# Decayed running sum behind a matmul: x's first two chunks loaded by halves of channels instead of halves of time

## The chip, the cores and the metric

The kernel runs on one core of a Trainium2 chip. The metric is the device time of one execution in microseconds, as the median of several runs. A core has five engines that work side by side, each through its own instructions in order: TensorE (PE, the matrix unit; PEld is its weight load), VectorE (DVE), ScalarE (ACT), GpSimd (POOL) and SyncE (SP). Transfers between the chip's main memory (HBM) and the core's memory (SBUF) are issued by some of these engines and carried out by 16 DMA engines. Matmul results go to PSUM, a memory of eight banks of 512 float32 columns for each of 128 partitions.

## The reference

```python
B, S, D = (16, 2048, 1024)            # x (B, S, D), w (D, D), decay (D), all float32
xw = x @ w
out[:, 0, :] = xw[:, 0, :]
for t in range(1, S):
    out[:, t, :] = decay[None, :] * out[:, t - 1, :] + xw[:, t, :]
```

So there are 16 independent sequences of 2048 steps. Each step is multiplied by a 1024 x 1024 matrix, and then a first-order recurrence with one decay for each output channel runs along time.

## The kernel before

**Chunks.** Time is cut into chunks of TL = 512 steps; there are 64 chunks in all. For each chunk the kernel forms the transposed product, with 128 output channels on the partitions and 512 steps along the row. Two chunks next to each other of one sequence make a group. A *step* (or slot) of the main loop is one group and one of the K = 8 blocks n of 128 output channels. It takes 2 x 8 matmuls of 128 x 128 weights by 512 columns, and its result fills a tile `ps` of 1024 columns (two PSUM banks). There are three such tiles, and two single banks called `spare`.

**Loading x.** The 1024 input channels are cut into NQ = 4 quarters of CQ = 256 channels. `load` (L101) fetches one quarter q of a chunk by a DMA on POOL's queue: 32 partitions (step modulo 32), NJ = 16 blocks of 32 steps, 256 channels. The DMA converts float32 to bf16 on the way. The tile `xb` holds the chunk with (quarter, step in the block) on the 128 partitions and (block j, channel) along the row. There are three `xb` tiles, used in turn, so the load of chunk c + 3 waits until chunk c has been transposed.

**Transposing x.** `turn` (L110) runs VectorE's 32 x 32 transpose over pairs of bf16 values taken as float32. The result `xw` has channel pairs on the partitions and is indexed [m, j, i, e]: m = 0 to 3 counts groups of channel pairs, (j, i) is the time, and e is the even or the odd channel of a pair. Contraction index k = 2m + e. `part` (L119) separates even and odd into `xt`, whose rows are contiguous in time; a matmul can also read `xw` directly with a stride of two (`pairs` in `matmul`, L125).

**Loading w.** `load_w` (L321) fetches w by half h of the output channels and parity e of the input channel, four DMAs each; `settle` (L328) and `settle_slots` (L376) copy it into `wsb` in the order that the matmuls want. Part (h, e) = (0, 0) comes first, over SP's and ACT's queues. The other three, called U0, U1, U2 here, go over POOL's queue.

**The order of the work.** Each engine works in the order in which the code records its instructions. A written agenda gives that order: entry -99 is the start, entries 0 to 33 follow steps 0 to 33, and later steps follow a rule. Each word of it is a letter and a number:

- M i loads half i of the first two chunks (M0 and M1 are chunk 0, M2 and M3 chunk 1), U i a part of w, and L the next quarter load from a list that starts with chunk 2 and grows by chunk c + 3 whenever chunk c is transposed.
- E i transposes one m of one half in time, and F i and G i copy it to `xt` on VectorE and on ACT: i = 0 to 3 is chunk 0's first half in time with m = 0 to 3, 4 to 7 its second half, and 8 to 15 the same for chunk 1.
- w i and W i settle a piece of w on ACT and on VectorE, q and Q on VectorE in two parts. K q copies one value of quarter q's load to a `gate` tile; warm-up matmuls that read the gate follow.
- T c transposes a whole later chunk; X c and Y c copy its m = 0, 1 and m = 2, 3 to `xt` on ACT.
- For a step s that is "paired": p and g copy its `ps` tile to SBUF on ACT (the whole to `xs`, and the even columns times decay to `h`), j adds on POOL, S scans on VectorE, h prepares the other half on ACT and c fills it in on POOL. `xs` has three buffers, so the p of the third paired step from then on waits for c. For a step that is not paired, S scans straight out of PSUM. B transposes a result for the store, which goes over SP's queue.

All of POOL's DMA issues share eight completion semaphores in turn, so that a load waits on POOL for the landing of the load eight places before it.

**The first steps.** Steps 0 to 3 are done together (L630 to L649). Chunk 0 goes into `firsts`, four banks: the four even k for the first half in time (256 columns), the same for the second half, and the odd k with 512 columns. Chunk 1 goes into `seconds` in two halves of 256 columns. From step 4 on all matmuls have 512 columns; step 8 (L669) does the blocks of steps 8 and 9 together.

Of the kernel before, what the change touches and what calls it, by code (L numbers as in the profile page):

```python
# [9 lines left out]
FP32 = mybir.dt.float32  # L10
BF16 = mybir.dt.bfloat16
# [3 lines left out]
def _ap(ap_obj: bass.AP, new_ap, extra_offset=0):  # L15
    return dataclasses.replace(
        ap_obj,
        ap=[list(p) for p in new_ap],
        offset=ap_obj.offset + extra_offset,
    )  # L20
# [5 lines left out]
def kernel(  # L26
# [26 lines left out]
    nc = tc.nc  # L53
    pin = tc.keep_in_program_order
    B, S, D = x.shape
# [3 lines left out]
    P = 32  # L59
    CQ = D // NQ  # L60
    K = CQ // P
    M = K // 2
    TL = 512
    NJ = TL // P
# [6 lines left out]
    sb = ctx.enter_context(tc.tile_pool(name="sb", bufs=1))  # L71
# [4 lines left out]
    def ring(pool, name, count, shape, dtype=FP32):  # L76
        i = turns[name] = turns.get(name, -1) + 1
        return pool.tile(shape, dtype, name=f"{name}{i % count}")

    def quad(q):  # L80
        return slice(q * P, (q + 1) * P)

    chunks = [(b, c * TL) for b in range(B) for c in range(NC)]
# [13 lines left out]
    xb_of = {}  # L97
    xw_of = {}
    xt_of = {}

    def load(c, q, j0=0, j1=NJ):  # L101
        b, t0 = chunks[c]
        if c not in xb_of:
            xb_of[c] = ring(sb, "xb", 3, [128, NJ, CQ], BF16)
        pin(nc.gpsimd.dma_start(  # L105
            out=xb_of[c][quad(q), j0:j1],
            in_=_ap(x, [[D, P], [P * D, j1 - j0], [1, CQ]],
                    (b * S + t0 + j0 * P) * D + q * CQ)))

    def turn(c, j0=0, j1=NJ, m0=0, m1=M):  # L110
        if c not in xw_of:
            xw_of[c] = ring(sb, "xw", 2, [128, M, NJ, P, 2], BF16)
        src = xb_of[c][:, j0:j1].rearrange("p j c -> p (j c)").bitcast(FP32)
        dst = xw_of[c].rearrange("p m j i e -> p (m j i e)").bitcast(FP32)
        pin(nc.vector.transpose(  # L115
            out=dst.rearrange("p (m j i) -> p j m i", m=M, i=P)[:, j0:j1, m0:m1],
            in_=src.rearrange("p (j m c) -> p j m c", m=M, c=P)[:, :, m0:m1]))
# [7 lines left out]
    def matmul(ps, n, k, xt, t0=0, t1=TL, start=0, pairs=None):  # L125
        if pairs is None:
            rhs = xt[:, k // 2, k % 2, t0:t1]
        else:
            rhs = pairs[:, k // 2, t0 // P:t1 // P, :, k % 2].rearrange("p j i -> p (j i)")
        lhs = wsb[:, k, n].rearrange("p q i -> p (q i)")  # L130
        pin(nc.tensor.matmul(  # L131
            out=ps[:, t0:t1] if ps.shape[1] >= t1 else ps,
            lhsT=lhs,
            rhs=rhs,
            start=(k == 0 and t0 == start),
            stop=(k == K - 1),
        ))
# [213 lines left out]
    H = NJ // 2  # L351
    halves = ((0, H), (H, NJ))
    for q in range(NQ):
        pin(nc.sync.dma_start(
            out=rows[q * P:q * P + R],
            in_=_ap(decay, [[P, R], [CH, 2], [1, P]], q * CR)))
    cols = const.tile([128, 2, P], FP32, name="cols")

    def load_half(i):
        for q in range(NQ):  # L360
            load(i // 2, q, *halves[i % 2])

    def spin_on(q):
        pin(nc.scalar.copy(out=gates[q][quad(q), 0:1], in_=xb_of[0][quad(q), 0, 0:1]))
# [44 lines left out]
    def bank(some, r, spot):  # L409
        both = psp.tile([128, len(some), NQ, 2, P], FP32, name=spot)  # L410
        for i in some:
            banks[i, r] = both, i - some[0]
# [22 lines left out]
    def half_slot(s, half, spot=None):  # L435
        tile_ = tiles[s % len(slots)]
        if spot is not None:
            tile_.ps.append(psp.tile([128, TL], FP32, name=spot)[:, 0:TL // 2])
        t = half * TL // 2
        for k in range(K):  # L440
            matmul(tile_.ps[half], tile_.n, k, xt_of[nch - 1], t, t + TL // 2, t)
# [35 lines left out]
    def turn_and_load(c):  # L477
# [44 lines left out]
        "L": lambda i: load(*loads.pop(0)) if loads else None,  # L522
    }
    agenda = {
        -99: "M0 M1 U0 M2 M3 U1 U2 w0 W1 w2 W3 K0 K1 K2 K3 E0 E1 G0 E2 G1 E3 F2 G3 E4 E5 G4 E6 G5 E7 F6 G7 q4 w5 Q4 W6 W7 D E8 E9 G8 E10 G9 E11 F10 G11 E12 L E13 G12 L E14 G13 E15 L F14 G15",
        0: "p0 z0 W8 W9 W10 W11",
        1: "g0",
        2: "L S1 L",
# [76 lines left out]
    def rest(s):  # L605
        do = [f"S{s - 1}"] if tiles[s - 1].paired else []
        do.append(f"C{s - 1}")
        if tiles[s - 2].paired:
            do.append(f"B{s - 2}")
        return do + [f"B{s - 1}"] + later.get(s, []) + ["L"] * len(loads)  # L610

    def perform(do):
        for deed in do:
            deeds[deed[0]](int(deed[1:] or 0))
# [3 lines left out]
    for step, (g, n) in enumerate(slots):  # L618
        T = TL * len(g)
        left = step - len(slots)  # L620
        if n % R == 0:
            ns, nj = range(n, n + R), T // P
            if left == -2 * R:
                outlets = [Outlet(ns, H, half) for half in range(2)]
            else:
                pieces = 1 if left < -7 * R else 2 if left < -6 * R else nj // H
                outlets = [Outlet(ns, nj, pieces=pieces, parts=2 if left == -5 * R else 1)]
        if left == -R:
            outlets = []
        if step == 0:  # L630
            heads = [ring(psp, "ps", 3, [128, T]) for _ in range(3)]
            firsts = [ps[:, 0:TL] for ps in heads] + [spares[0]]
            seconds = [ps[:, TL:T] for ps in heads] + [spares[1]]
            for j0, j1 in halves:
                for k in range(0, K, 2):
                    for i in range(R):
                        matmul(firsts[i], i, k, xt_of[0], j0 * P, j1 * P, pairs=xw_of[0])
            for k in range(1, K, 2):
                for i in range(R):
                    matmul(firsts[i], i, k, xt_of[0])  # L640
            for k0 in range(0, K, 2):
                for i in range(R):
                    for k in (k0, k0 + 1):
                        matmul(seconds[i], i, k, xt_of[1], 0, H * P,
                               pairs=xw_of[1] if k0 < 4 else None)
            for i in range(R):
                for k in range(K):
                    matmul(seconds[i], i, k, xt_of[1], H * P, TL, H * P,
                           pairs=xw_of[1] if i < 2 else None)  # L649
        if step < R:  # L650
            ps = heads[n] if n < 3 else tuple(spares)
        else:
            if step == K + 1:
                ps = nexts
            elif -R <= left < -1:
                ps = ring(psp, "ps", 3, [128, TL])
                spots.append(f"ps{turns['ps'] % 3}")
                if left == -2:
                    ps = [ps[:, 0:TL // 2]]
            elif len(g) == 2 or n % R < 3:  # L660
                ps = ring(psp, "ps", 3, [128, T])
            elif left == -1:
                ps = [ring(psp, "spare", 1, [128, TL])[:, 0:TL // 2]]
            else:
                ps = ring(psp, "spare", 1, [128, TL])
            todo = [(k, l) for k in range(K) for l in range(len(g))]
            if step < K:
                todo.sort(key=lambda kl: kl[0] % 2)
            elif step == K:  # L669
                todo = []  # L670
                nexts = (ring(psp, "spare", 1, [128, TL]), ring(psp, "ps", 3, [128, TL]))
                for l in range(len(g)):
                    for i, half in enumerate((ps[:, l * TL:(l + 1) * TL], nexts[l])):
                        for k in range(K):
                            matmul(half, n + i, k, xt_of.get(g[l]),
                                   pairs=xw_of[g[l]] if g[l] in (3,) else None)
            elif step == K + 1:
                todo = []
            if left >= -2:
                todo = []  # L680
            if 40 <= step < 190:
                pin(nc.tensor.nop(hint="x", nofuse=True))
            for k, l in todo:
                matmul(ps[:, l * TL:(l + 1) * TL], n, k, xt_of[g[l]])
        tiles.append(Tile(g, n, ps, outlets))
        if left >= -2:
            half_slot(left, 0)
        if left == -1:
            half_slot(-2, 1, spots[0])
            bank((0, 1), 0, "spare10")  # L690
        do = agenda.get(step, agenda.get(left) if left >= -20 else None)
        if do is None:
            do = usual(step)
        else:
            do = do.split()
            if left == -20:
                do = rest(step) + do
        perform(do)
# [29 lines left out]
```

## Time and profile before

| | |
|---|---|
| median of 3 runs | 903.84 us (903.73 to 904.28) |
| profiled execution, its own time | 903.68 us |
| span of its instructions | 901.9 us |
| granted TensorE clock | 1.00 |
| busy: PE, DVE, ACT, POOL | 892.0, 825.6, 687.6, 657.0 us |
| 512-column matmuls into `ps` from `xt` | 3934, mean 378 ns with overlap |
| x half loads (128 KB written) | 16, median 5.7 us to landing |
| x quarter loads (256 KB written) | 248, median 7.8 us to landing |
| w loads over POOL's queue | 12, median 5.1 us to landing |

A busy time counts overlapping matmuls once, while a mean of one matmul includes its overlap with its neighbours. The distance between two matmul starts is read from the chain. Sizes of transfers are those of the bf16 that is written, and the float32 that is read is twice as much. "Under 512 B" in the packet line counts the 4-byte completions as well.

In views of the chain and the timeline the columns are the start in us, the duration in us, and what ran; in the timeline the brackets tell how long the engine was idle before it and what ended that. In views of waits the numbers are the total in us, how often, and the longest. In the table of engines they are the busy time, its share of the span and the number of instructions.

### The profile page before, as it was taken

The page shows a single profiled execution, that of the slowest core. Times are in us where ns is not written, and L with a number is a line of the kernel's source. Part 1 is how long each engine was busy: PE and PEld are TensorE (multiplying, and loading weights), DVE is VectorE, ACT ScalarE, POOL GpSimd, SP SyncE. Part 2 cuts the span into 40 slices and gives each one's busy share as a digit, 9 for nine tenths or more (in the row PEclk, how much of TensorE's full clock was granted, in tenths as well). Part 3 has the DMA queues.
Part 4 walks back from the last instruction along what each step waited for, and adds up shares of the span by engine and source line. Part 5 has one row for each costly group of instructions (what it writes and reads, how often), then busy time and mean ns, then how long its engine had stood idle before and what let it go on. Part 6 is the DMA issues. An engine that isn't in the chain of part 4 may idle for free.

```text
span 901.9 us, 12226 instructions
## 1 busy us (share of the span) xinstructions
PE 892.0 (99%) x4127; PEld 412.1 (46%) x4209; DVE 825.6 (92%) x636; ACT 687.6 (76%) x962; POOL 657.0 (73%) x755
## 2 busy tenths in 40 slices
PE   9999999999999999999999999999999999999998
PEld 5544444444444444444444444444444444444444
DVE  4999999999999999999998999999999999999998
ACT  4889867777877877878778778777787787787743
POOL 7888678777767768777677687777777777776532
PEclk9999999999999999999999999999999999999999
DMA  9999999999999999999999999999999999999768
GB/s 193 196 215 217 231 218 217 215 240 253 254 249 252 248 249 252 242 247 230 225 234 228 224 228 228 233 228 228 232 229 228 227 230 225 228 226 222 176 152 234
DMA packets 403182, 204.77 MB, mean 227 GB/s; under 512 B 9392, under 2 KB 402096, under 8 KB 403120
## 3 DMA queue, kind: packets, MB, share of 16 engines
q1 hardware_dynamic: 265808, 134.77, 60.9%
q0 software_dynamic: 137024, 68.70, 56.7%
q8 instruction: 33, 0.54, 0.2%
q10 hardware_dynamic: 288, 0.52, 0.2%
q14 instruction: 29, 0.24, 0.1%
HBM read 138.42 MB, written 134.22 MB: 302 GB/s over the span
## 4 chain that ended last, share of the span: by engine, by line
PE 97%; DMA 1%; issue 1%; POOL 0%; DVE 0%; ACT 0%; DVEq 0%; POOLq 0%
PE ps L131 96%; PE spare L131 1%; DMA xb<-in_x_dram 1%; DMA ot<-in_w_dram 1%; POOL ot L323 0%; DVE so L233 0%; PE ps L419 0%; PE spare L419 0%; ACT xb L426 0%; DVE wsb L379 0%; DVEq L379 0%; POOLq L712 0%
## 5 line engine op out<-in xcount | busy, mean ns | idle before, releaser
L131 PE MATMUL ps<-xt,wsb 128*128 128x512 bf16 x3934 | 860.8, 378 | 4.7 <-DVE wsb L379 0.4
L131 PEld LDWEIGHTS <-wsb 128*128 128x128 bf16 x4160 | 406.8, 98 | 478.7 <-ACT wsb L330 0.8
L208 POOL TENSOR_TENSOR xs<-h,xs 128x512 f32<-128x512 f32 (+1 forms) x190 | 243.0, 1279 | 189.8 <-ACT h L169 84.6
L186 ACT COPY xs<-ps 128x1024 f32<-128x1024 f32 (+1 forms) x190 | 188.9, 994 | 156.9 <-PE ps L131 146.3
L283 DVE STREAM_TRANSPOSE ot<-so 128x1024 f32<-128x1024 f32 (+2 forms) x265 | 300.4, 1172 | 2.5 <-POOL so L202 1.1
L266 POOL TENSOR_TENSOR so<-h,xs 128x512 f32<-128x512 f32 (+1 forms) x190 | 241.5, 1273 | 41.2 <-ACT h L169 27.0
L123 ACT COPY xt<-xw 128x2048 bf16<-128x2048 bf16 (+1 forms) x136 | 242.3, 1790 | 7.6 <-DVE xw L115 7.4
L105 POOL DMA_DIRECT2D xb<-in_x_dram x264 | 174.3, 661 | 3.0 <-POOLq L712 0.9
L169 ACT ACTIVATE h<-so,dec 128x512 f32<-128x512 f32 (+1 forms) x190 | 145.4, 766 | 25.5 <-DVE so L213 22.3
L115 DVE STREAM_TRANSPOSE xw<-xb 128x2048 f32<-128x2048 f32 (+1 forms) x78 | 147.3, 1900 | 5.3 <-DMA xb<-in_x_dram 5.3
L213 DVE TENSOR_TENSOR_SCAN so<-spare,keep,xs 128x512 f32<-128x512 f32 (+1 forms) x97 | 120.0, 1240 | 27.6 <-POOL xs L208 27.2
L213 DVE TENSOR_TENSOR_SCAN so<-spare,xs 128x512 f32<-128x512 f32 x93 | 113.3, 1220 | 27.2 <-POOL xs L208 24.4
L169 ACT ACTIVATE h<-ps,dec 128x512 f32<-128x512 f32 (+1 forms) x189 | 129.5, 685 | 0.0
L233 DVE TENSOR_TENSOR_SCAN so<-dec,ps 128x1024 f32<-128x1024 f32 x34 | 76.9, 2261 | 0.8 <-ACT h L169 0.6
L233 DVE TENSOR_TENSOR_SCAN so<-dec,keep,ps 128x1024 f32<-128x1024 f32 (+2 forms) x35 | 74.8, 2140 | 0.0
L270 ACT COPY keep<-so 128x1 f32<-128x1 f32 x136 | 25.4, 189 | 9.1 <-DVE so L233 8.6
L204 ACT COPY so<-keep 128x1 f32<-128x1 f32 x97 | 18.4, 191 | 2.4 <-DVE ot L283 2.2
L131 PE MATMUL spare<-xt,wsb 128*128 128x512 bf16 (+1 forms) x64 | 12.9, 332 | 0.0
L131 PE MATMUL ps<-xw,wsb 128*128 128x256 bf16 (+1 forms) x68 | 11.2, 301 | 0.0
L202 POOL MEMSET so<- 128x1 f32 x93 | 10.7, 117 | 0.6 <-DVE ot L283 0.6
L323 POOL DMA_DIRECT2D ot<-in_w_dram x12 | 6.5, 546 | 3.2 <-DMA xb<-in_x_dram 1.9
L348 PE MATMUL spare<-idle 128*128 128x512 bf16 x22 | 6.8, 483 | 1.2 <-DVE idle L338 1.2
(40 smaller groups left out, 40.5 us busy)
## 6 DMA issues: line engine op xcount, KB each, us to landing
out_dram<-ot SPq DMA_DIRECT2D x236, 512.0 KB, 10.8
xb<-in_x_dram POOLq DMA_DIRECT2D x248, 256.0 KB, 7.8
out_dram<-ot SPq DMA_DIRECT2D x56, 128.0 KB, 2.6
xb<-in_x_dram POOLq DMA_DIRECT2D x16, 128.0 KB, 5.7
out_dram<-ot SPq DMA_DIRECT2D x8, 256.0 KB, 4.5
ot<-in_w_dram POOLq DMA_DIRECT2D x12, 128.0 KB, 5.1
out_dram<-xb SPq DMA_DIRECT2D x4, 256.0 KB
ot<-in_w_dram ACTq DMA_DIRECT2D x2, 256.0 KB, 5.1
```

Source lines behind the costliest of these rows:

```text
L105: pin(nc.gpsimd.dma_start(out=xb_of[c][quad(q), j0:j1], in_=_ap(x, [[D, P], [P * D, j1 - j0], [1, CQ]], (b * S + t0 + j0 * P) * D + q * CQ)))
L115: pin(nc.vector.transpose(out=dst.rearrange("p (m j i) -> p j m i", m=M, i=P)[:, j0:j1, m0:m1], in_=src.rearrange("p (j m c) -> p j m c", ...
L123: pin(copy(out=xt_of[c][:, m0:m1, :, j0 * P:j1 * P], in_=src))
L131: pin(nc.tensor.matmul(out=ps[:, t0:t1] if ps.shape[1] >= t1 else ps, lhsT=lhs, rhs=rhs, start=(k == 0 and t0 == start), stop=(k == K - 1),))
L169: pin(nc.scalar.activation(out=h, in_=src, func=mybir.ActivationFunctionType.Copy, scale=dec[:, self.n:self.n + 1]))
L186: pin(nc.scalar.copy(out=self.xs[:, i * size:(i + 1) * size], in_=ps))
L208: pin(nc.gpsimd.tensor_tensor(out=odds, in0=self.g, in1=odds, op=ALU.add))
L213: pin(nc.vector.tensor_tensor_scan(out=so[:, 3:T + 2:2], data0=squares[-1][:, n:n + 1].to_broadcast([128, T // 2]), data1=self.xs[:, 1:T:2 ...
L233: pin(nc.vector.tensor_tensor_scan(out=so[:, t + 2:t + 2 + size], data0=dec[:, n:n + 1].to_broadcast([128, size]), data1=ps, initial=befor ...
L266: pin(nc.gpsimd.tensor_tensor(out=self.so[:, 2:T + 2:2], in0=self.h, in1=self.xs[:, 0:T:2], op=ALU.add))
L270: pin(nc.scalar.copy(out=self.keep, in_=self.so[:, self.T + 1:self.T + 2]))
L283: pin(nc.vector.transpose(out=outlet.ot[:, j:j + size, c0:c0 + P], in_=self.so[:, t1:t1 + size * P].rearrange("p (i t) -> p i t", t=P)))
```

## The change

The first two chunks are cut in another direction. M0 loads channels 0 to 127 of each quarter for all 512 steps of chunk 0, and M1 channels 128 to 255. M2 and M3 do so for chunk 1. `load_side` takes the place of `load` for this; the tile is read as [side, j, channel] for these chunks, and `turn` takes its source from there. The sixteen DMAs carry the same bytes. Each row that is read is 512 B long instead of 1 KB, and there are twice as many.

The E, F and G of the agenda's entry -99 keep their number and size and get another order, since M0 now brings m = 0, 1 of both halves in time and M1 brings m = 2, 3. One L is added at the end of the entry, so that each later L takes the load that the next one took before.

The matmuls of steps 0 to 3 change from 96 with 256 columns and 16 with 512 to 8 with 256 columns (chunk 0, k = 0) and 60 with 512. Chunk 1 runs k = 0 to 3 for all four blocks out of `xw`, and then k = 4 to 7 block by block.

On ACT, VectorE and SP the kinds and the number of instructions stay as they are. On POOL the number stays, and the loads from chunk 2 on stand one place earlier among the other work.

```diff
--- before.py
+++ after.py
@@ -107,9 +107,30 @@
             in_=_ap(x, [[D, P], [P * D, j1 - j0], [1, CQ]],
                     (b * S + t0 + j0 * P) * D + q * CQ)))
 
+    def load_side(c, q, side):
+        b, t0 = chunks[c]
+        if c not in xb_of:
+            xb_of[c] = ring(sb, "xb", 3, [128, NJ, CQ], BF16)
+        wide = CQ // 2
+        dst = xb_of[c].rearrange("p j c -> p (j c)").rearrange(
+            "p (g j c) -> p g j c", g=2, c=wide)
+        pin(nc.gpsimd.dma_start(
+            out=dst[quad(q), side],
+            in_=_ap(x, [[D, P], [P * D, NJ], [1, wide]],
+                    (b * S + t0) * D + q * CQ + side * wide)))
+
     def turn(c, j0=0, j1=NJ, m0=0, m1=M):
         if c not in xw_of:
             xw_of[c] = ring(sb, "xw", 2, [128, M, NJ, P, 2], BF16)
+        if c < 2:
+            src = xb_of[c].rearrange("p j c -> p (j c)").bitcast(FP32)
+            src = src.rearrange("p (g j m c) -> p g j m c", g=2, j=NJ, c=P)
+            dst = xw_of[c].rearrange("p m j i e -> p (m j i e)").bitcast(FP32)
+            for m in range(m0, m1):
+                pin(nc.vector.transpose(
+                    out=dst.rearrange("p (m j i) -> p m j i", m=M, i=P)[:, m, j0:j1],
+                    in_=src[:, m // 2, j0:j1, m % 2]))
+            return
         src = xb_of[c][:, j0:j1].rearrange("p j c -> p (j c)").bitcast(FP32)
         dst = xw_of[c].rearrange("p m j i e -> p (m j i e)").bitcast(FP32)
         pin(nc.vector.transpose(
@@ -358,7 +379,7 @@
 
     def load_half(i):
         for q in range(NQ):
-            load(i // 2, q, *halves[i % 2])
+            load_side(i // 2, q, i % 2)
 
     def spin_on(q):
         pin(nc.scalar.copy(out=gates[q][quad(q), 0:1], in_=xb_of[0][quad(q), 0, 0:1]))
@@ -522,7 +543,7 @@
         "L": lambda i: load(*loads.pop(0)) if loads else None,
     }
     agenda = {
-        -99: "M0 M1 U0 M2 M3 U1 U2 w0 W1 w2 W3 K0 K1 K2 K3 E0 E1 G0 E2 G1 E3 F2 G3 E4 E5 G4 E6 G5 E7 F6 G7 q4 w5 Q4 W6 W7 D E8 E9 G8 E10 G9 E11 F10 G11 E12 L E13 G12 L E14 G13 E15 L F14 G15",
+        -99: "M0 M1 U0 M2 M3 U1 U2 w0 W1 w2 W3 K0 K1 K2 K3 E0 E4 G0 E1 G4 E5 F1 G5 E2 E6 G2 E3 G6 E7 F3 G7 q4 w5 Q4 W6 W7 D E8 E12 G8 E9 G12 E13 F9 G13 E10 L E14 G10 L E11 G14 E15 L F11 G15 L",
         0: "p0 z0 W8 W9 W10 W11",
         1: "g0",
         2: "L S1 L",
@@ -631,22 +652,19 @@
             heads = [ring(psp, "ps", 3, [128, T]) for _ in range(3)]
             firsts = [ps[:, 0:TL] for ps in heads] + [spares[0]]
             seconds = [ps[:, TL:T] for ps in heads] + [spares[1]]
-            for j0, j1 in halves:
-                for k in range(0, K, 2):
+            for k in range(0, K, 2):
+                for j0, j1 in halves if k == 0 else ((0, NJ),):
                     for i in range(R):
                         matmul(firsts[i], i, k, xt_of[0], j0 * P, j1 * P, pairs=xw_of[0])
             for k in range(1, K, 2):
                 for i in range(R):
                     matmul(firsts[i], i, k, xt_of[0])
-            for k0 in range(0, K, 2):
+            for k in range(M):
                 for i in range(R):
-                    for k in (k0, k0 + 1):
-                        matmul(seconds[i], i, k, xt_of[1], 0, H * P,
-                               pairs=xw_of[1] if k0 < 4 else None)
+                    matmul(seconds[i], i, k, xt_of[1], pairs=xw_of[1])
             for i in range(R):
-                for k in range(K):
-                    matmul(seconds[i], i, k, xt_of[1], H * P, TL, H * P,
-                           pairs=xw_of[1] if i < 2 else None)
+                for k in range(M, K):
+                    matmul(seconds[i], i, k, xt_of[1], pairs=xw_of[1] if i < 2 else None)
         if step < R:
             ps = heads[n] if n < 3 else tuple(spares)
         else:
```

## The prediction

> **What bounds the kernel now.** I read the page's shares and chain first, then who TensorE waited for, then the chain and the timeline of the first 45 us, where the change lies.
>
> ```profile
> PE 892.0 (99%) x4127; PEld 412.1 (46%) x4209; DVE 825.6 (92%) x636; ACT 687.6 (76%) x962; POOL 657.0 (73%) x755
> DMA packets 403182, 204.77 MB, mean 227 GB/s; under 512 B 9392, under 2 KB 402096, under 8 KB 403120
> PE 97%; DMA 1%; issue 1%; POOL 0%; DVE 0%; ACT 0%; DVEq 0%; POOLq 0%
> ```
>
> TensorE (PE) is busy 99% and 97% of the chain is its matmuls. So only two things can move the end: when its unbroken run begins, and any new gap after that. All its waits over the whole execution:
>
> ```profile
> PE spare L348 <- DVE idle L338: 1.2, 1, 1.2
> PE spare L348 <- ACT gate L364: 0.4, 1, 0.4
> PE ps L131 <- DVE wsb L379: 0.4, 1, 0.4
> ```
>
> The first two stand in front of warm-up matmuls. The third is the one that counts, and the chain of the first 32 us shows what it hangs on:
>
> ```profile
> 1.31 6.39 DMA xb<-in_x_dram
> ...
> 9.79 4.88 DMA ot<-in_w_dram
> ...
> 14.79 0.21 DVE wsb L379
> ...
> 15.04 0.39 PE ps L131
> ```
>
> The odd rows of w (U0) are issued behind the eight half loads of x's first chunk (M0, M1) and land at 14.67; VectorE settles them and the odd-k matmuls start at 15.04. From there PE does not stop. Between 2 and 42 us the transfer engines never run dry, so bytes or packets put ahead of U0 are paid by the whole kernel.
>
> The timeline of the same stretch, and that of ACT and POOL from 25 us on:
>
> ```profile
> 12.21 1.43 DVE L115 STREAM_TRANSPOSE xw<-xb 128x256 f32<-128x256 f32 x4 [0.89 <-DMA xb<-in_x_dram]
> 17.53 1.42 DVE L115 STREAM_TRANSPOSE xw<-xb 128x256 f32<-128x256 f32 x4 [1.35 <-DMA xb<-in_x_dram]
> 18.51 0.84 PE L131 MATMUL ps<-xw,wsb 128*128 128x256 bf16 x6
> 23.61 1.04 DVE L330 COPY wsb<-ot 128x512 bf16<-128x512 bf16 x4 [1.65 <-DMA ot<-in_w_dram]
> 25.63 6.67 PE L131 MATMUL ps<-xt,wsb 128*128 128x512 bf16 x29
> ...
> 25.96 1.30 POOL L208 TENSOR_TENSOR xs<-h,xs 128x512 f32<-128x512 f32 x1
> 32.96 2.56 POOL L266 TENSOR_TENSOR so<-h,xs 128x512 f32<-128x512 f32 x2
> 34.30 1.01 ACT L186 COPY xs<-ps 128x1024 f32<-128x1024 f32 x1 [0.71 <-POOL so L266]
> 36.05 3.70 ACT L123 COPY xt<-xw 128x2048 bf16<-128x2048 bf16 x2
> ```
>
> To be seen here: the first transposes of each half start when a load lands; the second chunk's matmuls run from 18.51 to 25.63; and ACT's copy p5 waits for a fill on POOL, with the copies of chunk 2 (X2, Y2) right behind it.
>
> **The price of a packet.** Each half load now has 512 packets of 512 B read and 256 B written, where it had 256 of 1 KB and 512 B. The trace has no such packet, so I take the distance between the landings of loads that follow one another in the busy stretch: 0.679 us for a half load of x (16 packets per engine and a 4-byte completion), 1.338 for a full one (32 and a completion), 0.651 for a load of w (8 packets of 2 KB read, 1 KB written, and a completion). The first two give 41.2 ns a packet and 20.5 a completion; the third 78.8 ns for the packet twice as long. The line through both, 3.6 ns and 37.6 per 512 B written, gives 22.4 ns for the new one. A new half load is then 32 x 22.4 + 20.5 = 0.737 us, 0.058 more. Bounds: the lower is no price beyond the bytes (20.6 ns), 0 more. Above stand the output stores, which also read 512 B: 676 of them in the busiest microsecond on 16 engines, 23.7 ns, so 0.10 more; about 500 in the stretches near the end that hold stores alone, 32 ns, so 0.37 more; and a price by count alone, 41.2 ns, 0.66 more. I take 22.4, since it comes from the same queue, direction and conversion.
>
> The Trainium skill, "DMA: Bandwidth & Descriptors", section "Why small descriptors are slow (HBM only)", gives 3 cycles over one per 32 B for each packet; with the same page's 850 MHz that makes, as an estimate, 41.2 ns for 1 KB, 78.8 for 2 KB and 22.4 for 512 B. By that rule the trace agrees at both measured sizes, and the sum would be the same.
>
> **The head.** Eight loads lie before U0: 8 x 0.058 = +0.46, odd phase at 15.50. Above it lies cover. The even matmuls shrink from 32 at 0.113 to 8 at 0.113 and 12 at 0.216 (3.61 to 3.49 us), but now k=4 needs both halves in time of a channel pair: M1 lands so that E2 starts at 12.21 + 0.46 = 12.67, E6 ends at 13.4, and 8 matmuls of 0.216 after that end at 15.1. Still 0.4 before U0, so the stall on w absorbs this; were U0 early, this would cost instead. Sixteen issues on POOL cost 0.65 us instead of 0.58 (rows of full and half loads); POOL sat idle 1.95 us ahead of U0 waiting for a landing, which hides it. The 16 transposes keep number and size.
>
> **The second chunk.** The 16 odd matmuls of 0.216 end at 15.50 + 3.47 = 18.97. M2 is 12 loads late: the first transpose at 17.53 + 0.70 = 18.23, and 512 columns need E8 and E12, so 0.36 + 0.40 later, 18.99, with the handover 19.02: +0.05. M3 (16 loads late) gives E10 and E14 at 21.16 + 0.76 = 21.9; PE wants them at 19.02 + 3.45 = 22.5, covered. The matmuls themselves: 64 in 7.12 us become 32 of 0.216, 6.91: -0.21. PE leaves this chunk 0.46 + 0.05 - 0.21 = +0.30 late, at 25.93.
>
> **Behind it.** U1 and U2 come 16 x 0.058 = 0.93 later. U1's last landing (23.5) becomes 24.4; the four settles W8 to W11 end at 25.6, before 25.93. U2 (25.83) becomes 26.76, when ACT reaches w12 anyway (26.45 + 0.3). But POOL works in order, and the extra L at the end of the first agenda entry puts one more load (0.65 us) ahead of j0. Its loads also wait for landings of U1 and U2: the fourth, at 23.77 today, goes at 24.7. So j0 goes from 25.96 to 27.55, and with it j2, j4 and the fill c0, whose end goes from 34.25 to about 35.85. p5 on ACT waits for that fill (same xs buffer): +1.6, then g5, X2, Y2. Y2 ends at 39.75 today; VectorE's T2 (0.93 late, 36.95) is not last, and ACT was 0.15 ahead of it, so Y2 ends at about 41.25. PE's step 8 starts at 39.45, runs four matmuls with X2's part and wants Y2 at 40.3: slack 0.55 now. 1.5 - 0.55 = 0.95: this, and no longer 0.30, is PE's delay from here on. Further on the shifted L makes the load for chunk 6 wait on POOL for T3 (it reuses that buffer) ahead of j5, so VectorE's scan S7 ends some 1.95 later, at 46.8; step 10 needs its bank at 46.4 + 0.95, covered. Later steps have looser waits (S11 ends 2.9 before its bank is wanted).
>
> Sum: +0.95 on a span of 901.9 (profiled execution 903.68), thus 904.6; the median of the runs is 0.16 above that execution, so 904.8 at most; I say 904.7. The delay by Y2 moves by 16 times the extra time of one half load, so the packet's price decides everything. A difference of 0.2%, 1.8 us, is about what a measurement can tell from no change; it is reached when 16 loads cost 1.8 us, at 24.1 ns a packet.
>
> **Rivals.** (1) Slower: short packets are not as cheap as the line says. Place: the 16 half loads; it decides from 24.1 ns. At the stores' 32 ns it is 5.9 us, near 909.7. For: the rows with stores alone. Against: those were another queue writing to HBM, and they reached 23.7 in mixed stretches. Chance 0.30 for 24.1 to 35 ns.
>
> (2) Slower still: a packet written in 256 B costs as much as one of 512 B. Then 16 x 0.66 = 10.5 us, 914.4. For: no packet from this queue ever came closer than 41 ns except the completions. Against: w's packets scale with bytes, which count alone would not do; the 128 B packets of decay took about 13 to 26 ns. Chance 0.13. The Trainium skill, same page, section "Specifications", names 512 B as the least transfer for line rate, with a read-modify-write below; no run so far shows its price, and the decay rows speak against a large one.
>
> (3) The new placing is harmless: POOL's shift does not reach Y2, or the packets cost nothing more (or are not shortened at all, with the packet count left at 403182). Then PE's -0.21 and the head's 0 to +0.46 remain: 903.6 to 904.1. For: the fetch of instructions that made U1 late at 21.4 us may fall elsewhere, giving POOL back 0.65 us. Against: POOL's order is fixed and busy there. Chance 0.11.
>
> (4) Faster by over 1.8 us: would need U0 earlier, and the wait before it was only 0.4 us. Chance 0.05.
>
> The forecast itself gets 0.41. Slower is (1) and (2) plus 0.03 of the forecast's upper end: 0.46. Same is the rest of the forecast and (3): 0.49. The range reaches from (3), 903.4, up to the upper part of (1), 910.5, leaving out (2) and a little at the bottom.
>
> **What would show it.** The page should have 407278 packets, 17584 under 512 B (8192 more), and 44 fewer PE matmuls. Right: w's chain piece landing near 15.1 and the odd phase near 15.5; step 4 near 25.9; a PE wait on ACT's xt of about half a microsecond at 40.6. Wrong: half loads landing over 0.78 us apart (rival 1 or 2), PE waits on xw at 19 or 22.5, no gap at 40 (rival 3), or any PE gap after 50 us.

## The result, and the profile after

The changed kernel takes 906.60 us (906.21 to 907.61, 7 runs) where the one before takes 903.84 in runs on the same chip: 1.0033 times as long, interval 1.0021 to 1.0045. A second series of the same kernel gave 906.93, ratio 1.0038 (1.0026 to 1.0050). It is slower by 0.3%: 2.8 us where 0.9 were forecast, and past the 0.2% that a measurement can tell from no change. The profiled execution took 906.6 us with a span of 904.8, 2.9 us more than the span before.

The page's lines on engines, packets and the chain:

```profile
PE 892.8 (99%) x4083; PEld 408.1 (45%) x4165; DVE 826.0 (91%) x636; ACT 687.5 (76%) x962; POOL 658.1 (73%) x755
DMA packets 407278, 204.77 MB, mean 226 GB/s; under 512 B 17584, under 2 KB 406192, under 8 KB 407216
PE 86%; DVE 4%; issue 3%; DMA 3%; POOL 2%; ACT 1%; DVEq 0%; ACTq 0%; POOLq 0%
```

The packets are the 407278 that were forecast, 8192 more of them short, and there are 44 fewer matmuls. The chain has changed its kind. Before, it was 97% matmuls; now 11 points have gone to VectorE, POOL, transfers and issues, because followed backwards it leaves TensorE at 114.2 us for a copy of ACT that ended just then, and runs through the other engines from there. TensorE did not stop at that place, so these points do not measure lost time; the waits do. Two waits of TensorE are new among all its waits (total in us, how often, the longest):

```profile
PE ps L152 <- ACT xt L144: 1.1, 2, 0.8
PE ps L152 <- DVE xw L130: 0.9, 1, 0.9
```

The timeline of the head shows the second of them (here and below, rows between those shown are left out):

```profile
12.97 1.42 DVE L130 STREAM_TRANSPOSE xw<-xb 128x256 f32<-128x256 f32 x4 [1.21 <-DMA xb<-in_x_dram]
13.80 0.84 PE L152 MATMUL ps<-xw,wsb 128*128 128x512 bf16 x3 [0.86 <-DVE xw L130]
...
15.10 0.36 DVE L400 COPY wsb<-ot 128x128 bf16<-128x128 bf16 x2 [0.39 <-DMA ot<-in_w_dram]
15.60 0.81 PE L152 MATMUL ps<-xt,wsb 128*128 128x512 bf16 x3
18.26 1.42 DVE L130 STREAM_TRANSPOSE xw<-xb 128x256 f32<-128x256 f32 x4 [1.70 <-DMA xb<-in_x_dram]
19.08 0.84 PE L152 MATMUL ps<-xw,wsb 128*128 128x512 bf16 x3
```

The odd phase starts at 15.60 without a bracket: nothing held it but the even matmuls before it, while both of w's copies in the row before end at 15.46. TensorE had stood 0.86 us at 13.80 for the transposes of M1. The timeline further on shows the first wait of the list and what leads to it:

```profile
26.89 1.30 POOL L229 TENSOR_TENSOR xs<-h,xs 128x512 f32<-128x512 f32 x1
...
31.71 0.64 POOL L105 DMA_DIRECT2D xb<-in_x_dram  x1 [0.36 <-DMA xb<-in_x_dram]
33.91 0.65 POOL L105 DMA_DIRECT2D xb<-in_x_dram  x1 [1.55 <-issue]
34.57 1.30 POOL L229 TENSOR_TENSOR xs<-h,xs 128x512 f32<-128x512 f32 x1
35.82 2.54 POOL L287 TENSOR_TENSOR so<-h,xs 128x512 f32<-128x512 f32 x2
37.14 1.01 ACT L207 COPY xs<-ps 128x1024 f32<-128x1024 f32 x1 [3.40 <-POOL so L287]
38.63 3.70 ACT L144 COPY xt<-xw 128x2048 bf16<-128x2048 bf16 x2
40.59 1.02 PE L152 MATMUL ps<-xt,wsb 128*128 128x512 bf16 x4 [0.33 <-ACT xt L144]
42.38 1.02 PE L152 MATMUL ps<-xt,wsb 128*128 128x512 bf16 x4 [0.77 <-ACT xt L144]
```

The fill on POOL (35.82, before 32.96) lets ACT's p5 go at 37.14 instead of 34.30; the copies X2 and Y2 behind it end at 42.33 instead of 39.75, and TensorE waits for both at step 8. In the row at 33.91 POOL stood 1.55 us and the profile names nothing for the last part of it. The chain of the first 46 us shows how long:

```profile
24.06 8.71 DMA xb<-in_x_dram
32.77 1.14 issue
33.91 0.35 POOL xb L105
```

The load that uses the same semaphore eight places earlier landed at 32.77, and the next one was issued 1.14 us after that. Other loads that wait in this way go 0.28 us after the landing.

To follow the delay through the kernel I compare the start of the same weight load, counted from the last one, with the execution before. This lag is 0.62 us from step 5 up to step 8, 2.04 behind step 8, and 2.04 still at the last matmul. The span is longer by 2.92, so another 0.88 us comes behind TensorE.

### The profile page after: what moved, and what is told of

It is laid out like the page before. It is cut to its first block, busy times and chain, and to the rows that moved or that the text cites. A ratio compares the mean times of both kernels' runs of the same rounds, so it can differ in the third digit from the quotient of the medians.

```text
span 904.8 us, 12141 instructions
## 1 busy us (share of the span) xinstructions
PE 892.8 (99%) x4083; PEld 408.1 (45%) x4165; DVE 826.0 (91%) x636; ACT 687.5 (76%) x962; POOL 658.1 (73%) x755
## 2 busy tenths in 40 slices
DMA packets 407278, 204.77 MB, mean 226 GB/s; under 512 B 17584, under 2 KB 406192, under 8 KB 407216
## 4 chain that ended last, share of the span: by engine, by line
PE 86%; DVE 4%; issue 3%; DMA 3%; POOL 2%; ACT 1%; DVEq 0%; ACTq 0%; POOLq 0%
PE ps L152 85%; DMA xb<-in_x_dram 3%; DVE xw L136 1%; DVE ot L304 1%; DVE so L234 1%; PE spare L152 1%; DVE so L254 1%; POOL ot L344 1%; POOL xb L117 1%; POOL xb L105 0%; POOL xs L229 0%; ACT xt L144 0%; ACT h L190 0%; POOL so L287 0%; PE ps L440 0%
## 5 line engine op out<-in xcount | busy, mean ns | idle before, releaser
L152 PE MATMUL ps<-xt,wsb 128*128 128x512 bf16 (+1 forms) x3921 | 859.6, 379 | 5.4 <-ACT xt L144 1.1
L152 PEld LDWEIGHTS <-wsb 128*128 128x128 bf16 x4116 | 402.5, 98 | 484.9 <-issue 2.8
L136 DVE STREAM_TRANSPOSE xw<-xb 128x2048 f32<-128x2048 f32 x62 | 141.6, 2284 | 0.0
L152 PE MATMUL ps<-xw,wsb 128*128 128x512 bf16 (+1 forms) x50 | 12.5, 374 | 0.9 <-DVE xw L130 0.9
L130 DVE STREAM_TRANSPOSE xw<-xb 128x256 f32<-128x256 f32 x16 | 5.7, 413 | 6.5 <-DMA xb<-in_x_dram 6.5
```

The costliest lines, as they stand in the source:

```text
L136: pin(nc.vector.transpose(out=dst.rearrange("p (m j i) -> p j m i", m=M, i=P)[:, j0:j1, m0:m1], in_=src.rearrange("p (j m c) -> p j m c", ...
L152: pin(nc.tensor.matmul(out=ps[:, t0:t1] if ps.shape[1] >= t1 else ps, lhsT=lhs, rhs=rhs, start=(k == 0 and t0 == start), stop=(k == K - 1),))
```

## The experiments

Four questions were put: whether packets and the extra L together make the wait at step 8 (theory A), where the 0.88 us at the end come from (theory B: a fetch of TensorE's own instructions, which takes a transfer engine away from the last stores), how much the new order of the head costs by itself (theory C), and, later, what holds the load at 33.91 (theory H). All kernels but one were timed against the one before; lags are in us, of one profiled execution each, against the profiled execution before.

| kernel | median, ratio to before | lag before / after step 8 | span minus before |
|---|---|---|---|
| changed | 906.60, 1.0033 (1.0021 to 1.0045) | 0.62 / 2.04 | 2.9 |
| changed, again | 906.93, 1.0038 (1.0026 to 1.0050) | 0.98 / 1.67 | 2.7 |
| without the extra L | 905.01, 1.0015 (1.0006 to 1.0024) | 0.91 / 0.91 | 0.9 |
| before, with the extra L | 904.41, 1.0007 (0.9998 to 1.0016) | 0.41 / 0.60 | 1.1 |
| 15 blocks | 905.08, 1.0015 (1.0006 to 1.0024) | 0.54 / 0.54 | 1.4 |
| 256-column matmuls | 905.89, 1.0026 (1.0017 to 1.0034) | 1.08 / 2.43 | 2.4 |
| 256 columns, no extra L | 905.06, 1.0012 (1.0003 to 1.0020) | 1.31 / 1.68 | 1.7 |
| 15 blocks, no extra L | 904.50, 1.0009 (1.0000 to 1.0018) | 0.15 / 0.15 | 0.9 |
| 14 blocks | 904.07, one run | 0.05 / 0.38 | 0.4 |
| three short loads | 906.71, 1.0034 (1.0022 to 1.0047) | 0.95 / 2.18 | 2.6 |
| six short loads | 905.60, 1.0019 (1.0010 to 1.0027) | 1.46 / 2.19 | 2.6 |
| before, w by rows | 906.55, 1.0032 (1.0021 to 1.0044) | 2.72 / 2.72 | 2.7 |

**The extra L taken out, and put alone into the kernel before.**

```diff
 agenda entry -99 of the changed kernel
-... E11 G14 E15 L F11 G15 L
+... E11 G14 E15 L F11 G15
```

> The changed kernel without the one L added at the end of the first agenda entry; loads by channels, packets and matmuls stay as changed. Theory A (PE's 1.42 us of waiting at step 8 comes from POOL, where one more load stands ahead of the adds j0 to j4 and the fills, on top of packets that make U1, U2 and chunk 2 land 0.93 us later): j0, j2, j4 and the first fill move forward by at least 0.65 us, VectorE no longer loses time before S5, PE's waits at step 8 fall from 1.4 to 0.2 to 0.7 us, and the time to about 905.7 us. Theory B (88 fewer TensorE instructions move TensorE's 16 KB instruction fetches to 28.1 and 890.2 us, where they hold up one DMA ring under chunk 2's loads and under the last stores): nothing changes, 906.6. Theory C (the start itself, where a chunk's matmuls wait for both halves in time, is what is lost): nothing changes, 906.6.

```diff
 agenda entry -99 of the kernel before
-... G13 E15 L F14 G15
+... G13 E15 L F14 G15 L
```

> The kernel before with nothing but the added L at the end of the first agenda entry. Theory A: the order on POOL alone moves j0, j4 and the first fill 0.65 to 0.9 us later, the copy Y2 as much, against a slack of 0.55 us: PE waits 0.1 to 0.4 us at step 8, 903.9 to 904.3 us; without the longer packets the extra load costs little. Theory B and theory C: no change, 903.84.

Without the L the wait at step 8 is gone, where 0.2 to 0.7 us of it were expected to stay. In the timeline of that kernel the fill lets p5 go two microseconds earlier, and X2 and Y2 with it:

```profile
33.81 2.54 POOL L287 TENSOR_TENSOR so<-h,xs 128x512 f32<-128x512 f32 x2
35.14 1.02 ACT L207 COPY xs<-ps 128x1024 f32<-128x1024 f32 x1 [1.08 <-POOL so L287]
36.63 3.70 ACT L144 COPY xt<-xw 128x2048 bf16<-128x2048 bf16 x2
```

The L alone on the kernel before moves p5 to 35.70, and TensorE's lag grows by 0.19 us at step 8. That is little, and so is its whole effect (the interval of the ratio holds 1). It has a cost that I had not forecast. At step 16 TensorE waits for a bank whose scan on VectorE has come late, and the lag grows from 0.60 to 1.15:

```profile
68.42 3.83 PE L131 MATMUL ps<-xt,wsb 128*128 128x512 bf16 x16 [0.39 <-DVE so L233]
```

**Fewer packets.** The loads of the first two chunks leave out the last one or two of their 16 blocks of 32 steps, and zeros stand there. Each block left out takes away 16 packets per DMA engine ahead of U0.

```diff
-            out=dst[quad(q), side],
-            in_=_ap(x, [[D, P], [P * D, NJ], [1, wide]],
+            out=dst[quad(q), side, 0:NJ - 1],
+            in_=_ap(x, [[D, P], [P * D, NJ - 1], [1, wide]],
```

> The changed kernel with 15 of the 16 time blocks of each half load of the first two chunks (the last 32 steps of these chunks are not loaded and stand at zero), so that a half load takes 30 packets an engine instead of 32: 30 x 22.4 + 20.5 = 692 ns, against 679 before the change and 736 with it. Nothing else changes but two small memsets while VectorE is idle. Theory A: 16 loads give back 0.72 us of the transfers' delay of 0.93; the odd phase starts 0.3 earlier, PE's waits at step 8 fall by 0.4 or more, 905.6 to 905.9 us. Theory B: 906.6, since the fetches stay where they are. Theory C: only the odd phase's 0.3, 906.3.

With 15 blocks and the extra L kept, TensorE does not wait at step 8 at all, and the median is 905.08, below the 905.6 to 905.9 expected. So taking away the L or a sixteenth of the packets each removed all of the wait in its execution. That does not show that the wait needs both. Each edit also ends the 1.14 us hold of the load at 33.91, which is treated below, and a smaller wait comes back in kernels that lack one of the two: with 14 blocks, and at 256 columns without the L. What is shown is the path, POOL's fill and p5 and Y2 behind it.

> The changed kernel without the added L and with 15 of 16 time blocks in the first two chunks' loads (the last 32 steps of these chunks are not loaded and stand at zero), so that a half load takes 692 ns instead of 736, almost the 679 of before. What is left of the change is the order: both halves in time must be transposed before a 512-column matmul. If the late start of the odd phase (0.5 to 0.6 us) comes from the packets' price, PE is 0.1 to 0.3 late and the time 903.8 to 904.2 us, plus what the end adds; if it comes from the order (k=4 waits for two transposes behind M1, and eight matmuls of 0.226 us follow), 0.4 to 0.6 stays, 904.2 to 904.6 us plus what the end adds.

> The changed kernel with 14 of 16 time blocks in the first two chunks' loads (the last 64 steps of these chunks are not loaded and stand at zero): a half load takes 28 x 22.4 + 20.5 = 648 ns, less than before the change. With the loads' lateness gone and the added L kept, the theory of both together expects no wait or under 0.3 us at step 8. The load that POOL issued 0.8 us after its semaphore was ready was the fortieth in two runs and the forty-first in the run with 15 blocks; if that hold goes by the number of descriptors issued to a DMA engine (about 1030 in each), it now falls on the forty-second; if it goes by the time or the kernel's place, it stays on the fortieth or vanishes.

With both taken away, the lag is 0.15 us in the whole run of matmuls. With 14 blocks and the L kept it is 0.05 up to step 8, and then 0.38: p5 goes at 35.48 as with 15 blocks, and TensorE, which comes half a microsecond earlier, waits for Y2 again. So theory C, a cost of the new order by itself, gets no support. It is not excluded below some 0.4 us either: the kernel before with the extra L, whose head is unchanged, was 0.41 us late in its execution.

**The matmuls at 256 columns again.** Forty-four of the 512-column matmuls are cut in two, so that TensorE has as many instructions as before.

```diff
-                    matmul(seconds[i], i, k, xt_of[1], pairs=xw_of[1])
+                    for j0, j1 in halves:
+                        matmul(seconds[i], i, k, xt_of[1], j0 * P, j1 * P, pairs=xw_of[1])
 ... and likewise for chunk 0 and for k = 4 to 6 of chunk 1
```

> The changed kernel with its loads and its order, but 44 of the 512-column matmuls of steps 0 to 3 split into two of 256 columns, so that TensorE has as many instructions as before the change. Theory A: the waits at step 8 stay near 1.4 us; the matmuls of the second chunk, which read two-byte values at a stride of two at 0.226 us for 512 columns, cost the same in two halves of 0.113; the time stays within 0.3 us of 906.6. Theory B: the fetches go back to about 21 and 879 us, the last landing comes 0.86 us earlier behind the last copy, and chunk 2's loads have no late ring: 904.7 to 905.7 us. Theory C: narrow matmuls start on the first half, but both halves land together here, so 906.6.

> The changed kernel with both edits taken together: without the added L, and with 44 of the matmuls split, so that TensorE has as many instructions as before. What is left of the change is the loads by channels with their short packets and the order of the first two chunks. Theory A (packets and the added L together make the wait at step 8): no wait at step 8, PE 0.6 to 1.0 us late from the odd phase on, 904.3 to 904.8 us. Theory B (a TensorE instruction fetch among the last stores adds up to 0.9 us at the end in some executions): no fetch there now, so the span ends as late as PE does, and the median is 0.2 to 0.5 below that of the run without the L alone; if the end plays no part, the two medians agree.

With the L kept, the wait at step 8 is there (0.25 and 0.77 us), so it does not come from the widths. Without the L the expectation of no wait failed:

```profile
PE ps L152 <- ACT xt L144: 0.2, 1, 0.2
```

The lag grows by 0.37 us there. U2 had landed at 27.65 us in that execution (26.01 in the changed kernel), and POOL's j0 had started at 28.15.

The lag at the end of TensorE's work is larger with the L kept than in the changed kernel, 2.43, and yet the profiled execution ends 0.5 us earlier, because nothing is added behind the last matmul. That speaks for theory B. The page's queue line `q8 instruction` has 33 packets of 16 KB. I take them for TensorE's instructions, since they move when TensorE's instructions change in number. In the packet records the last of them starts near 880 us in every kernel with 4209 weight loads and near 889 in those with 4165. Where it falls near 889 and takes 1.26 to 1.56 us instead of the usual 0.95, the span is longer by another 0.45 to 0.98 us: six executions. In two executions it falls there and takes 0.95 to 0.96, and nothing is added. In two others it takes 1.31 and 1.35 but near 880, and nothing is added either. So a long fetch near 889 goes with the late end in every profile. Which of the two causes the other is not shown, and why the fetch is sometimes long is open. The medians of the two kernels without the extra L (905.01 wide, 905.06 narrow) show no difference, so how often runs pay for it is open too.

**The held load.** The same kernel again, to see what repeats:

> The changed kernel unaltered, to tell what belongs to the program from what belongs to one execution. Theory A (packets and the extra L push the fill on POOL so late that step 8 waits for chunk 2's copies): the fill still ends beyond 36.5 us and TensorE waits at step 8 by 1.0 us or more in all; the median stays 1.5 to 3.5 us above before. If the hold of the load at 33.9 us (0.86 us for which the profile names nothing) belongs to the program, a hold of 0.5 us or more is seen again on the same load; if it is chance, it is gone and the wait at step 8 is 0.3 to 0.8 us smaller, near the 0.65 that was forecast. Theory B (TensorE's late fetch of instructions stretches the last stores): the span again ends 0.6 to 1.0 us later than TensorE's lag alone explains; if that too is chance, within 0.2 us of it.

The hold repeats to the hundredth: the load is issued at 33.52, 1.14 us after its landing at 32.39. So does the late end (0.98). The wait at step 8 is 0.5 us, where 1.0 or more was expected, and the lag grows by 0.69 there. The three executions with the hold so far had one thing in common: counted from the start, the packets that POOL's queue had given each DMA engine (33 for a whole half load, completion included, 9 for w, 33 for a quarter) pass 1024 with just this load. The next two kernels move that place by a few packets only.

```diff
+        nj = NJ - 1 if side == 1 and c == 1 and q < 3 else NJ       # three short loads
+        nj = NJ - 1 if c == 1 and (side == 1 or q < 2) else NJ      # six short loads
-            out=dst[quad(q), side],
-            in_=_ap(x, [[D, P], [P * D, NJ], [1, wide]],
+            out=dst[quad(q), side, 0:nj],
+            in_=_ap(x, [[D, P], [P * D, nj], [1, wide]],
```

> The changed kernel, but the last three half loads of the second chunk leave out the last of their 16 blocks of time (zeros stand there), which takes 2 packets per DMA engine from each. The question is the hold of the load at 33.9 us, 1.14 us after the landing it waits for, on the 40th DMA of POOL's queue in three executions of this order and in none where the packets are fewer (15 or 14 blocks everywhere). Theory H (the hold falls on the load with which the packets issued per DMA engine pass 1024): through that load they are 1032 in the changed kernel and 1026 here, still past 1024, so the hold stays, 0.8 to 0.9 us beyond the usual 0.28, and the fill ends beyond 36.5. Rival (the hold comes from time lost to the packets, or from the late DMA engine): also stays, a little smaller. Median 1.5 to 3.5 us above before by both.

> The same with six half loads short by one block: 1020 packets per engine through the 40th DMA of POOL's queue, so only the next one passes 1024. Only three more blocks of 32 steps and 128 channels are left out than with three short loads, 0.13 us of transfers in all. Theory H: the hold is gone, the load goes 0.28 us after the landing it waits for, near 32.8, the fill ends near 36.1 instead of 37.1, and TensorE's wait at step 8 shrinks by 0.7 to 1.0 us, to between 0.2 and 0.8; median 0.5 to 1 us below that with three short loads. Rival (time lost to packets, or the late engine): the hold stays at 0.7 us or more and the two kernels agree within 0.3 us.

The chain of the first 46 us with three short loads (1026 packets through this load):

```profile
32.90 1.14 issue
34.03 0.51 POOL xb L105
```

and with six (1020):

```profile
33.78 0.28 issue
34.06 0.64 POOL xb L105
```

Theory H holds: the 1.14 becomes 0.28 when six packets fewer lie ahead, and the median falls by 1.1 us. The rest of its expectation failed in the profiled execution, the slowest of the eleven runs of this kernel: the landing itself came 0.88 us later, after a head that was 0.5 us later, so the fill ended at 37.26 instead of near 36.1 and p5 went at 37.30, as with three short loads.

Other kernels show the hold on other loads. With 15 blocks, with and without the L, the count passes 1024 at the forty-first load of POOL's queue (1033), and that load, which waits for chunk 2's transposes, went 1.18 and 1.17 us after their end. With w by rows, the last kernel below, the count passes at the forty-fifth (1037, if the additional packets are spread evenly), and it went 1.27 us after chunk 3's transposes. Where POOL waits for transposes without a hold, such loads go 0.29 to 0.31 us after. The timeline rows with 15 blocks, with the L and without it:

```profile
37.28 2.57 POOL L105 DMA_DIRECT2D xb<-in_x_dram  x4 [0.59 <-DVE ot L304]
36.88 2.56 POOL L105 DMA_DIRECT2D xb<-in_x_dram  x4 [0.98 <-DVE ot L304]
```

The brackets name what VectorE did last; the transposes had ended at 36.10 and 35.71. So the hold follows the count and not the place in the order or the time. What POOL waits for at this count is not shown. In the other six executions POOL worked right up to the load that passes 1024, and no hold is seen.

**A try to beat the kernel before.** U0 is what its odd phase waits for, and it comes in four DMAs by quarters. Here it comes in four DMAs by m, over all 128 partitions, so that k = 1 could be settled first.

```diff
+        if i == 0:
+            for m in range(M):
+                pin(nc.gpsimd.dma_start(
+                    out=stage[0, 1][:, m * CH:(m + 1) * CH],
+                    in_=_ap(w, [[CQ * D, NQ], [2 * D, P], [1, CH]],
+                            (2 * P * m + 1) * D)))
+            return
```

> The kernel before, but with U0 (the odd rows of w for the first half of the output) loaded in four DMAs by row group m, 128 partitions each, instead of four by quarter; the same bytes and packets. Each m can be settled when its own DMA lands, so that the odd phase need not wait for the last. If the landing of all of U0 is what PE waits for at 15.04 us, the odd phase follows the even one at 14.45, 0.5 to 0.6 us earlier, and of that 0.3 to 0.5 us should arrive at the end: 903.3 to 903.5 us. If something else is as late (M2's landing, the settles of w for the other half, Y2's slack of 0.55 us), 903.6 to 903.9.

It lost 2.7 us. The timeline shows the later pieces and chunk 1 coming late:

```profile
16.02 0.29 DVE L330 COPY wsb<-ot 128x512 bf16<-128x512 bf16 x1 [0.99 <-DMA ot<-in_w_dram]
17.99 0.29 DVE L330 COPY wsb<-ot 128x512 bf16<-128x512 bf16 x1 [1.68 <-DMA ot<-in_w_dram]
18.34 0.82 PE L131 MATMUL ps<-xt,wsb 128*128 128x512 bf16 x3 [0.61 <-DVE wsb L330]
21.23 0.84 PE L131 MATMUL ps<-xw,wsb 128*128 128x256 bf16 x6 [1.85 <-DVE xw L115]
```

Its page has 1536 more packets than before, all of 4 bytes: 384 more for each of the four DMAs. At 20.5 ns for each on 16 engines that is, as an estimate, 2.0 us, most of the loss. No version that was run beats the kernel before.

## Why the prediction was right and wrong

The direction of each step and the place of the wait came true: slower, through POOL's fill, ACT's p5 and Y2, at step 8. The total came out some 2 us above the forecast of 0.95. The lag of 2.9 us in the profile consists of 0.62 (head), 1.42 (step 8) and 0.88 (end), where I had 0.30, 0.65 and nothing. That the wait came at the forecast place is in part luck, since two errors on the way there had opposite signs.

**The packet's price** was right at the transfer engines. In the packet records the 4-byte completions of half loads start 0.735 us apart in the busy stretch (0.679 before, forecast 0.737), which is 22.3 ns a packet. The estimate by the Trainium skill, "DMA: Bandwidth & Descriptors", section "Why small descriptors are slow (HBM only)", was 22.4, and the trace agrees.

What the other engines wait for is the landing, though, and landings fell further behind. The second chunk's eight loads landed 0.777 us apart (15.81 to 21.25), and 0.777 to 0.786 apart in all five executions with whole loads; before it was 0.675. From the start of a load's completion packets to its landing it took 0.52 us for the first of these loads and 0.85 for the last (means over the 16 engines; 0.37 before for each). The loads of w that follow bring this back to 0.34. Why short packets land later is not shown. The Trainium skill, same page, section "Specifications", names a read-modify-write below 512 B; no run here shows whether it has a part in this. Taken by the landings, a packet would cost 23.6 to 23.9 ns, so rival 1, which begins at 24.1, falls narrowly, and rival 2 clearly.

**The head** failed at "still 0.4 before U0, so the stall on w absorbs this". I had M1 late by 8 times 0.058. The completion packets of M1's last quarter started 0.36 us later than before, no worse than that, but took 1.08 us to land instead of 0.42. In the execution before, the first eight loads landed 0.626 us apart (7.70 to 12.08), and after 0.735 (7.71 to 12.85). M1 is 0.77 late, not 0.46, E2 starts at 12.97 instead of 12.67, and the eight even matmuls behind it start 0.226 us apart instead of 0.216, so they end behind U0's settling. U0 itself landed 0.30 later than before (14.98), where I had 0.46.

**The second chunk's -0.21** was not there. Matmuls of 512 columns that read `xw` at a stride of two start 0.226 us apart, while I took 0.216 from those that read `xt`; 24 of the 32 are of the first kind. From 19.08 to 26.23 is 7.15 us, against 7.12 before.

How much of the head's 0.62 belongs to the change can't be said from one profile. The changed kernel's own heads were 0.62 and 0.98 us late in its two profiles, and the unchanged head of the kernel before with the extra L 0.41, with its M0 landing at 10.16 instead of 9.46.

**POOL's shift** was the right mechanism, mis-sized in two terms. j0 came at 26.89 and not 27.55: U2 landed at 26.01 instead of 26.76, and the fetch of instructions that stood at 21.1 us before, beside U1, now ran at 27.85, as rival 3 had said it might. From j0 to the end of the fill I had 8.30 us, as before, and it took 10.22. POOL stood idle for 1.91 us of it, where I had no wait. The extra L puts the fortieth load ahead of j4, which before had only the thirty-ninth ahead of it, and both waited for landings of chunk 2's quarters: 0.36 us for that at 31.43 and 0.69 for that at 32.77, which came 1.24 and 1.27 later than before. The remaining 0.86 is the hold, which no row before had shown. So the fill ended at 37.11 instead of 35.85, Y2 came at 42.33 instead of 41.25, and the wait was 1.42 instead of 0.65 us. The medians with three and with six short loads put the hold at about 1.1 us, of which the three further blocks left out can account for 0.13. With the hold gone, a wait of 0.73 us stayed in the profile, so the hold is not the whole of it. What was forecast for later steps held: the load for chunk 6 waits for T3 on POOL at 42.12, and neither step 10 nor a later one is delayed in the changed kernel.

**"Nothing at the end"** failed: 0.88 and 0.98 us in the two profiles. I had counted 44 fewer matmuls as nothing, and did not ask where the last fetch of instructions would fall; that it lengthens the end is likely and not shown.

Rival 3, the harmless placing, is not what happened: even without the extra L the kernel takes 905.01, where this rival ended at 904.1. Rival 4 had no support in any run.

## What to carry to other kernels

A queue that works in order can turn a small delay far ahead into a larger one behind: with a sixteenth of the packets less, or one load moved by a place, TensorE's wait of 1.4 us some 15 us later was gone. When a change makes packets shorter, count them in four ways: their time, how far their landings fall behind, the order that they push on the issuing engine, and where their running count falls. Cover ("0.4 us before U0") has to be worked out from the landings of the stage itself, not from a mean spacing of another stretch.

## What the runs showed of the hardware

- POOL held the load with which its packets per DMA engine passed 1024: it went 1.14 us after the landing that it waits for (four executions of three kernels, the fortieth load, 1026 to 1032 packets), or 1.17 to 1.27 us after the transposes that it waits for (three executions, the forty-first and the forty-fifth, 1033 and 1037). Without a hold these were 0.28 and 0.29 to 0.31 us; the fortieth load went 0.28 us after with 1020 packets or fewer.
- Half loads in packets of 256 B written left the transfer engines 0.735 us apart and landed 0.777 to 0.786 us apart, so that the time from completion packet to landing grew from 0.52 to 0.85 us over eight loads. With packets of 512 B it stayed at 0.37.
- A matmul of 512 columns took 0.226 us from one start to the next when it read every second bf16, 0.216 when it read them in a row; at 256 columns 0.113 and 0.110.
- The 16 KB packets that I take for fetches of TensorE's instructions take about 0.95 us each. In the changed kernel's first profile one ran at 27.85 us, and in the next five loads one completion came 0.9 to 1.2 us behind the others; in its second profile one ran at 26.75, and no such straggler followed.
- A DMA of 128 partitions with one row each left 400 packets of 4 bytes, where one of 32 partitions with four rows each left 16.
